# Adaptive max pooling: a nine-row ring, 48 KB load runs issued alternately from SyncE and ScalarE, 9 KB store runs, two early from GpSimd and the rest written last

## Chip, cores, metric

One core of one Trainium2 chip. The metric is the device time in microseconds; lower is better. Ratios are the mean time of one kernel's fast runs over that of the other's of the same rounds, so not quite the ratio of the medians that are quoted beside them. "Span" is the length of the profiled execution; the timed runs are about 2 us longer.

## The reference

```python
x: (32, 256, 4096) float32, output_size = 256
for i in range(256):
    result[:, :, i] = max(x[:, :, 16*i : 16*(i+1)], axis=-1)
```

There are 8192 rows of 16 KB. One "row" below means one row in each of the 128 partitions (2 MB), so the job is 64 such rows, 134.2 MB in and 8.4 MB out. Nothing is reused.

## The kernel before

Each load brings two rows (4 MB, 32 KB per partition) into one of three buffers. VectorE reduces each row in one instruction. The last four rows come in smaller loads with buffers of their own. Of 32 stores (256 KB each, 2 KB runs), 16 are kept back and queued on SyncE behind the body's loads, in three portions.

```python
for n in range(n_body):                              # 30 double rows
    t = in_pool.tile([P, R, O, W], fp32, tag="in")   # 3 buffers
    nc.sync.dma_start(out=t, in_=xt[n])
    o = new_out()
    for r in range(R):
        nc.vector.reduce_max(out=o[:, r*O:(r+1)*O], in_=t[:, r], axis=X)
    out_tiles[n] = o
    if n >= defer_start: deferred.append(n)
    else:                nc.scalar.dma_start(out=ot[n], in_=o)
emit_deferred(6)
# ... two single rows; 5 deferred stores; two rows in quarters; 5 deferred stores; the last store
```

Of the kernel before, what the change touches and what calls it, by code (L numbers as in the profile page):

```python
# [1 line left out]

# [4 lines left out]


@with_exitstack  # L10
def kernel(
    ctx: ExitStack,
    tc: tile.TileContext,
    x: bass.AP,
    output_size: bass.AP,
    out: bass.AP,
):
    nc = tc.nc

    B, C, L = x.shape  # L20
    O = int(output_size)
    assert L % O == 0, (L, O)
    W = L // O

    P = nc.NUM_PARTITIONS

    xf = x.flatten_outer_dims()
    of = out.flatten_outer_dims()
    rows = xf.shape[0]
    assert rows % P == 0  # L30

    fp32 = mybir.dt.float32

    R = 2
    IN_BUFS = 3
    CHUNKS_PER_ROW = 4
    N_CHUNK_ROWS = 2
    N_FULL_ROWS = 2
    DEF_A = 6
    DEF_B = 5  # L40
    DEF_C = 5

    while R > 1 and rows % (P * R) != 0:
        R //= 2
    nprow = rows // P
    nmacro = nprow // R
    n_chunks = CHUNKS_PER_ROW if O % CHUNKS_PER_ROW == 0 else 1
    oc = O // n_chunks

    n_tail_prow = min(N_CHUNK_ROWS + N_FULL_ROWS, nprow)  # L50
    n_chunk_prow = min(N_CHUNK_ROWS, n_tail_prow)
    n_tail_macro = -(-n_tail_prow // R)
    n_body = nmacro - n_tail_macro
    tail_start_prow = n_body * R
    n_defer = min(DEF_A + DEF_B + DEF_C, max(n_body - 1, 0))

    xt = xf.rearrange("(n p r) (o w) -> n p r o w", p=P, r=R, w=W)
    ot = of.rearrange("(n p r) m -> n p (r m)", p=P, r=R)

    in_pool = ctx.enter_context(tc.tile_pool(name="inpool", bufs=IN_BUFS))  # L60
    out_pool = ctx.enter_context(
        tc.tile_pool(name="outpool", bufs=min(nmacro, n_defer + 5))
    )

    out_tiles = {}
    deferred: list[int] = []

    def new_out():
        return out_pool.tile([P, R * O], fp32, tag="out", name="o")

    def emit_deferred(k):
        for _ in range(k):
            if deferred:
                m = deferred.pop(0)
                nc.sync.dma_start(out=ot[m], in_=out_tiles[m])  # L75

    defer_start = n_body - n_defer
    for n in range(n_body):
        t = in_pool.tile([P, R, O, W], fp32, tag="in")
        nc.sync.dma_start(out=t, in_=xt[n])  # L80
        o = new_out()
        for r in range(R):
            nc.vector.reduce_max(  # L83
                out=o[:, r * O : (r + 1) * O],
                in_=t[:, r],
                axis=mybir.AxisListType.X,
            )
        out_tiles[n] = o
        if n >= defer_start:
            deferred.append(n)  # L90
        else:
            nc.scalar.dma_start(out=ot[n], in_=o)

    emit_deferred(DEF_A)

    o = None
    last_n = nmacro - 1
    for q in range(tail_start_prow, nprow):
        n, r = divmod(q, R)
        if r == 0 or o is None:  # L100
            o = new_out()
            out_tiles[n] = o
        if q == nprow - n_chunk_prow:
            emit_deferred(DEF_B)
        if q < nprow - n_chunk_prow:
            tr = in_pool.tile([P, 1, O, W], fp32, tag="inrow", bufs=2)
            nc.sync.dma_start(out=tr, in_=xt[n][:, r : r + 1])
            nc.vector.reduce_max(  # L108
                out=o[:, r * O : (r + 1) * O],
                in_=tr[:, 0],  # L110
                axis=mybir.AxisListType.X,
            )
        else:
            for c in range(n_chunks):
                tl = in_pool.tile(
                    [P, oc, W], fp32, tag="inchunk", bufs=2 * n_chunks
                )
                nc.sync.dma_start(
                    out=tl, in_=xt[n][:, r, c * oc : (c + 1) * oc, :]
                )  # L120
                nc.vector.reduce_max(  # L121
                    out=o[:, r * O + c * oc : r * O + (c + 1) * oc],
                    in_=tl,
                    axis=mybir.AxisListType.X,
                )
        if r == R - 1 and n != last_n:
            nc.scalar.dma_start(out=ot[n], in_=o)

    emit_deferred(len(deferred))

    nc.scalar.dma_start(out=ot[last_n], in_=out_tiles[last_n])


# [1 line left out]
_INS = ['x', 'output_size']  # L135
_OUTS = [((32, 256, 256), 'float32')]
#: Inputs that are plain numbers.
_NUMBERS = {'output_size': 256}


# [26 lines left out]
```

## Time and profile before

| | before |
|---|---|
| time, median of 3 runs | 339.17 us |
| span of the profile | 336.9 us |
| moved | 142.6 MB, mean 423 GB/s |
| VectorE busy | 281.0 us |
| last load landed, by the trace's semaphore events | 332.2 us |

These are lines of the page of the kernel before: VectorE's busy time; its busy tenths, those of the DMA engines and the GB/s in 40 slices of the span; the packet count; and the main group of reductions (line, engine, operation, out<-in, count, busy us, ns of one, waiting before it and for what).

```profile
span 336.9 us, 241 instructions
...
DVE 281.0 (83%) x70; POOL 0.2 (0%) x4
...
DVE  0488988888988889888899888888988888898895
...
DMA  7999999999999999999999999999999999999997
GB/s 311 436 436 441 417 454 406 454 409 454 426 430 430 436 428 434 430 430 435 429 438 432 436 432 436 436 436 428 424 436 428 436 412 436 429 414 427 405 414 275
DMA packets 10370, 142.63 MB, mean 423 GB/s; under 512 B 1152, under 2 KB 1152, under 8 KB 6272
...
L83 DVE TENSOR_REDUCE o<-t 128x256 f32<-128x4096 f32 x60 | 262.4, 4414 | 50.5 <-DMA t<-in_x_dram 50.5
...
```

The DMA line is at 9 from the second slice to the last but one: the transfers bound this kernel. The chain of work that ended last seems to say something else, because it alternates between a load and two reductions. This is a piece of it, in order of time (start, us, what):

```profile
...
186.90 8.76 DVE o L83 x2
195.66 0.02 issue
195.67 20.34 DMA t<-in_x_dram
...
216.03 8.76 DVE o L83 x2
...
```

A load is issued when two reductions have freed its buffer, and it lands 20.3 us later. One load takes only 9.7 us of the engines (128 packets of 32 KB, 1213 ns each by the trace's packet records, over 16 engines); the rest of the 20.3 us is time behind the load in front of it. So the chain shows the return of a buffer, and the engines always have a load queued.

The end, in VectorE's timeline (start, us, engine, line, operation, out<-in, count, waiting before it):

```profile
...
318.22 4.42 DVE L108 TENSOR_REDUCE o<-tr 128x256 f32<-128x4096 f32 x1 [0.86 <-DMA tr<-in_x_dram]
322.79 5.00 DVE L121 TENSOR_REDUCE o<-tl 128x64 f32<-128x1024 f32 x4
328.34 5.06 DVE L121 TENSOR_REDUCE o<-tl 128x64 f32<-128x1024 f32 x4 [0.55 <-DMA tl<-in_x_dram]
```

The last two reductions are of the last quarters to land. VectorE ends at 333.4 us, 1.2 us after the last load. This gap is called the *backlog* below.

### The profile page before, as it was taken

The numbers are of one execution on the slowest core, as the hardware profiler recorded it, in microseconds if no ns is written. First come the engines' busy times: TensorE is split into PE (matmuls) and PEld (weight loads), VectorE is DVE, ScalarE is ACT, GpSimd is POOL, SyncE is SP. The second block draws the span as 40 slices with busy tenths as digits, with TensorE's granted clock in tenths as the row PEclk, the third lists the DMA queues.
The fourth block names the chain that finished last, engine by engine and source line by source line (L and its number), as shares of the span: only waits on it lengthen the run. The fifth ranks groups of instructions, "written<-read, shape, count | busy, mean of one in ns | idle before, by whom it ended". The sixth has DMA issues, their size and how long they took to land.

```text
span 336.9 us, 241 instructions
## 1 busy us (share of the span) xinstructions
DVE 281.0 (83%) x70; POOL 0.2 (0%) x4
## 2 busy tenths in 40 slices
DVE  0488988888988889888899888888988888898895
POOL 0000000000000000000000000000000000000000
DMA  7999999999999999999999999999999999999997
GB/s 311 436 436 441 417 454 406 454 409 454 426 430 430 436 428 434 430 430 435 429 438 432 436 432 436 436 436 428 424 436 428 436 412 436 429 414 427 405 414 275
DMA packets 10370, 142.63 MB, mean 423 GB/s; under 512 B 1152, under 2 KB 1152, under 8 KB 6272
## 3 DMA queue, kind: packets, MB, share of 16 engines
q1 hardware_dynamic: 8064, 138.42, 96.1%
q10 hardware_dynamic: 2304, 4.20, 3.2%
q14 instruction: 2, 0.02, 0.0%
HBM read 134.22 MB, written 8.39 MB: 423 GB/s over the span
## 4 chain that ended last, share of the span: by engine, by line
DMA 74%; DVE 24%; SPq 1%; issue 0%; DVEq 0%
DMA t<-in_x_dram 60%; DVE o L83 23%; DMA out_dram<-o 11%; DMA tl<-in_x_dram 3%; DVE o L121 1%; SPq L75 1%; SPq L80 0%; DVEq L83 0%
## 5 line engine op out<-in xcount | busy, mean ns | idle before, releaser
L83 DVE TENSOR_REDUCE o<-t 128x256 f32<-128x4096 f32 x60 | 262.4, 4414 | 50.5 <-DMA t<-in_x_dram 50.5
L121 DVE TENSOR_REDUCE o<-tl 128x64 f32<-128x1024 f32 x8 | 9.8, 1220 | 1.0 <-DMA tl<-in_x_dram 0.6
L108 DVE TENSOR_REDUCE o<-tr 128x256 f32<-128x4096 f32 x2 | 8.8, 4420 | 1.0 <-DMA tr<-in_x_dram 0.9
L148 POOL MEMSET const-bfloat16-1.0<- 128x1 bf16 x1 | 0.1, 102 | 0.0
L148 POOL MEMSET const-uint8-127<- 128x1 uint8 x1 | 0.1, 101 | 0.0
L148 POOL MEMSET const-float32-0.0<- 128x1 f32 x1 | 0.1, 99 | 0.2 <-issue 0.2
L148 POOL MEMSET const-float32-1.0<- 128x1 f32 x1 | 0.1, 98 | 0.0
## 6 DMA issues: line engine op xcount, KB each, us to landing
t<-in_x_dram SPq DMA_DIRECT2D x30, 4096.0 KB, 21.5
out_dram<-o ACTq DMA_DIRECT2D x16, 256.0 KB, 16.1
out_dram<-o SPq DMA_DIRECT2D x16, 256.0 KB, 14.0
tr<-in_x_dram SPq DMA_DIRECT2D x2, 2048.0 KB, 16.4
tl<-in_x_dram SPq DMA_DIRECT2D x8, 512.0 KB, 9.2
```

The costliest lines, as they stand in the source:

```text
L75: nc.sync.dma_start(out=ot[m], in_=out_tiles[m])
L83: nc.vector.reduce_max(out=o[:, r * O : (r + 1) * O], in_=t[:, r], axis=mybir.AxisListType.X,)
L108: nc.vector.reduce_max(out=o[:, r * O : (r + 1) * O], in_=tr[:, 0], axis=mybir.AxisListType.X,)
L121: nc.vector.reduce_max(out=o[:, r * O + c * oc : r * O + (c + 1) * oc], in_=tl, axis=mybir.AxisListType.X,)
L148: nc = _bacc.Bacc("TRN2", target_bir_lowering=False, num_devices=1)
```

## The change

The intent: longer runs (48 KB in, 9 KB out) for fewer packets; a ring of nine rows; load issues spread over two engines; a few early stores moved to GpSimd; the rest of the stores last. The core of it (set-up and the removed code cut):

```diff
-        nc.sync.dma_start(out=t, in_=xt[n])
+    queues = [nc.sync, nc.scalar]
+    for g in range(N_GROUPS):                      # 7 groups of 9 rows
+        sizes = LATE if g == N_GROUPS - 1 else [LOAD] * (G // LOAD)   # LATE = [3,2,2,1,1], LOAD = 3
+        for n in sizes:
+            queue = queues[n_loads % 2]
+            queue.dma_start(out=ring[:, at : at + n], in_=xg[g][:, r : r + n])
+            n_loads += 1
+            for i in range(n):
+                nc.vector.reduce_max(out=o[...], in_=ring[:, at + i], axis=X)
+        if g < N_GROUPS - 1 - HELD:                # HELD = 4
+            nc.gpsimd.dma_start(out=og[g], in_=o)
+        else:
+            held.append((og[g], o))
+    # ... the 64th row, in four pieces, from SyncE ...
+    for i, (dst, src) in enumerate(held):
+        queues[i % 2].dma_start(out=dst, in_=src)
+    nc.scalar.dma_start(out=ol, in_=last_out)
```

More of the change, by code (lines that the diff above doesn't have):

```diff
@@ L18 @@
     nc = tc.nc
+    P = nc.NUM_PARTITIONS
+    fp32 = mybir.dt.float32
     B, C, L = x.shape
@@ L23 @@
     W = L // O
-    P = nc.NUM_PARTITIONS
     xf = x.flatten_outer_dims()
@@ L29 @@
     rows = xf.shape[0]
-    assert rows % P == 0
-    fp32 = mybir.dt.float32
-    R = 2
-    IN_BUFS = 3
-    CHUNKS_PER_ROW = 4
-    N_CHUNK_ROWS = 2
-    N_FULL_ROWS = 2
-    DEF_A = 6
-    DEF_B = 5
-    DEF_C = 5
-    while R > 1 and rows % (P * R) != 0:
-        R //= 2
-    nprow = rows // P
-    nmacro = nprow // R
-    n_chunks = CHUNKS_PER_ROW if O % CHUNKS_PER_ROW == 0 else 1
-    oc = O // n_chunks
-    n_tail_prow = min(N_CHUNK_ROWS + N_FULL_ROWS, nprow)
-    n_chunk_prow = min(N_CHUNK_ROWS, n_tail_prow)
@@ L52 @@
-    n_tail_macro = -(-n_tail_prow // R)
-    n_body = nmacro - n_tail_macro
-    tail_start_prow = n_body * R
-    n_defer = min(DEF_A + DEF_B + DEF_C, max(n_body - 1, 0))
-    xt = xf.rearrange("(n p r) (o w) -> n p r o w", p=P, r=R, w=W)
-    ot = of.rearrange("(n p r) m -> n p (r m)", p=P, r=R)
-    in_pool = ctx.enter_context(tc.tile_pool(name="inpool", bufs=IN_BUFS))
-    out_pool = ctx.enter_context(
-        tc.tile_pool(name="outpool", bufs=min(nmacro, n_defer + 5))
-    )
-    out_tiles = {}
@@ L66 @@
-    deferred: list[int] = []
-    def new_out():
-        return out_pool.tile([P, R * O], fp32, tag="out", name="o")
-    def emit_deferred(k):
-        for _ in range(k):
-            if deferred:
-                m = deferred.pop(0)
-                nc.sync.dma_start(out=ot[m], in_=out_tiles[m])
-    defer_start = n_body - n_defer
-    for n in range(n_body):
-        t = in_pool.tile([P, R, O, W], fp32, tag="in")
-        nc.sync.dma_start(out=t, in_=xt[n])
-        o = new_out()
-        for r in range(R):
-            nc.vector.reduce_max(
-                out=o[:, r * O : (r + 1) * O],
-                in_=t[:, r],
-                axis=mybir.AxisListType.X,
-            )
-        out_tiles[n] = o
-        if n >= defer_start:
-            deferred.append(n)
-        else:
-            nc.scalar.dma_start(out=ot[n], in_=o)
@@ L94 @@
-    emit_deferred(DEF_A)
-    o = None
-    last_n = nmacro - 1
-    for q in range(tail_start_prow, nprow):
-        n, r = divmod(q, R)
-        if r == 0 or o is None:
-            o = new_out()
-            out_tiles[n] = o
-        if q == nprow - n_chunk_prow:
-            emit_deferred(DEF_B)
-        if q < nprow - n_chunk_prow:
-            tr = in_pool.tile([P, 1, O, W], fp32, tag="inrow", bufs=2)
-            nc.sync.dma_start(out=tr, in_=xt[n][:, r : r + 1])
-            nc.vector.reduce_max(
-                out=o[:, r * O : (r + 1) * O],
-                in_=tr[:, 0],
-                axis=mybir.AxisListType.X,
-            )
-        else:
-            for c in range(n_chunks):
-                tl = in_pool.tile(
-                    [P, oc, W], fp32, tag="inchunk", bufs=2 * n_chunks
-                )
-                nc.sync.dma_start(
-                    out=tl, in_=xt[n][:, r, c * oc : (c + 1) * oc, :]
-                )
+    assert rows == 64 * P
@@ new lines @@
+    RING = 9
+    G = 9
+    N_GROUPS = 7
+    LOAD = 3
+    LATE = [3, 2, 2, 1, 1]
+    HELD = 4
+    PIECES = 4
+    pool = ctx.enter_context(tc.tile_pool(name="pool", bufs=1))
+    ring = pool.tile([P, RING, O, W], fp32, tag="ring", name="ring")
+    outs = [
+        pool.tile([P, G * O], fp32, tag=f"out{i}", name=f"out{i}")
+        for i in range(N_GROUPS - 1)
+    ]
+    last_out = pool.tile([P, O], fp32, tag="lastout", name="lastout")
+    main = N_GROUPS * G * P
+    xg = xf[0:main].rearrange("(g p r) (o w) -> g p r o w", p=P, r=G, w=W)
@@ new lines @@
+    og = of[0:main].rearrange("(g p r) m -> g p (r m)", p=P, r=G)
+    xl = xf[main:rows].rearrange("p (o w) -> p o w", w=W)
+    ol = of[main:rows]
+    queues = [nc.sync, nc.scalar]
+    n_loads = 0
+    n_read = 0
+    held = []
+    for g in range(N_GROUPS):
+        o = outs[g % len(outs)]
+        sizes = LATE if g == N_GROUPS - 1 else [LOAD] * (G // LOAD)
+        r = 0
+        for n in sizes:
+            at = n_read % RING
+            queue = queues[n_loads % 2]
+            queue.dma_start(out=ring[:, at : at + n], in_=xg[g][:, r : r + n])
+            n_loads += 1
+            for i in range(n):
@@ L121 @@
                 nc.vector.reduce_max(
-                    out=o[:, r * O + c * oc : r * O + (c + 1) * oc],
-                    in_=tl,
+                    out=o[:, (r + i) * O : (r + i + 1) * O],
+                    in_=ring[:, at + i],
                     axis=mybir.AxisListType.X,
                 )
-        if r == R - 1 and n != last_n:
-            nc.scalar.dma_start(out=ot[n], in_=o)
-    emit_deferred(len(deferred))
-    nc.scalar.dma_start(out=ot[last_n], in_=out_tiles[last_n])
+            n_read += n
@@ new lines @@
+            r += n
+        if g < N_GROUPS - 1 - HELD:
+            nc.gpsimd.dma_start(out=og[g], in_=o)
+        else:
+            held.append((og[g], o))
+    at = n_read % RING
+    oc = O // PIECES
+    for c in range(PIECES):
+        cut = slice(c * oc, (c + 1) * oc)
+        nc.sync.dma_start(out=ring[:, at, cut], in_=xl[:, cut])
+        nc.vector.reduce_max(
+            out=last_out[:, cut], in_=ring[:, at, cut], axis=mybir.AxisListType.X
+        )
+    for i, (dst, src) in enumerate(held):
+        queues[i % 2].dma_start(out=dst, in_=src)
```

## The prediction, as put on record

> **What bounds the kernel now.** The transfers. The page gives 142.6 MB at a mean of 423 GB/s; its slices show DMA at 9 from the second to the last but one; the stretch view gives 431 GB/s from 20 to 160 us and 430 from 190 to 290. VectorE works 281.0 of 336.9 us; its 50.5 us of waiting are for loads. The chain names a load 22 us, then two reductions 8.76 us, but that is the release of a buffer: 22 us is two loads of 9.7 us and the rest of a third, so a full load is always queued. The Trainium skill ("DMA: Bandwidth & Descriptors", Where 436 GB/s comes from) states a ceiling of 435 GB/s; this trace agrees, at 432. So about 1% is to be had.
>
> **What a packet costs.** Medians in the trace: 32 KB 1213 ns, 16 KB 611, 4 KB 159, 2 KB 84, semaphore 9. They fit 9 ns + bytes / 27.2 GB/s. A 48 KB packet is then an estimated 1815 ns, a 9 KB one 348.
>
> **Sum over 16 engines.** Before: 3840 x 1213 + 256 x 611 + 1024 x 159 + 4096 x 84 + semaphores = 333 us. After: 2304 x 1815 + 128 x (1815 + 2 x 1213 + 2 x 611) + 512 x 159 + 896 x 348 + the last 1 KB runs = 330.4 us. Saved: 2.8 us, all critical, as the engines never idle. But 14 of the 32 stores already alternated on a second queue with load packets, and three loads with their stores took 30.95 us where the sum says 31.2 (without stores 29.1): overlap between queues already hides their 9 ns. That takes 1 us off the saving; two load queues may give as much back.
>
> **What else moves.**
> - Start: loads 0 and 1, on two queues, share the engines packet by packet, so both land at about 32 us, not one at 13. VectorE starts then; its 281 us still end before the loads. Ring slots come free after three reductions (13.2 us), at about 45.5 us; load 2 ends near 46.4, and issue to first packet takes 1.2 us. Gap of 0 to 1.5 us, once. Later VectorE (13.2 per 14.5 us load) gains ground; no further gaps.
> - End: before, the last stores trickle: engines lose 1.4 us in the last 3. After, the stores of groups 4 and 6 (1.18 MB, 2.8 us each) are still queued when the last piece is reduced, so the small last store hides. Gain about 1 us.
> - VectorE's work is unchanged: 64 rows at 4.41 us. The two GpSimd stores are early and hidden.
>
> **Prediction.** 339.2 - 1.8 (packets) + 0.7 (start gap) - 1.0 (end) - 1.0 (two load queues) = 336.0 us (rounded). Range 334.0 to 339.5. Chances: faster by over 2%: 0.02; within 2%: 0.93; slower: 0.05.
>
> **What would show each step.** 48 KB packets near 1815 ns, 9 KB near 348. First reduction near 32 us, not 13.3. One dip in the slices near 45 us. Mid-kernel 432 to 435 GB/s. No slice at the end as low as 275 GB/s. VectorE idle about 50 us still, mostly before its first reduction.
>
> **What would make it wrong.** If dependencies were kept for the whole ring, loads and reductions would take turns: far above 400 us. If the wider stride between partitions (144 KB, not 32) slowed the memory, the middle would fall below 425 GB/s. If VectorE, started 19 us later, never caught up, slots would come late again and again, and dips would repeat. If the held stores ran ahead of the last loads, the tail would be exposed.

## The result

353.30 us (median of 4 runs, 352.35 to 353.35) against 338.95 us before on the same chip: ratio 1.0415, 95% interval 1.0395 to 1.0434. The change is 4% slower; the prediction was 1% faster, and the time lies outside its range.

The page after, the same lines:

```profile
span 351.5 us, 179 instructions
...
DVE 278.0 (79%) x67; POOL 1.4 (0%) x6
...
DVE  0003999999939799498999905999886999299996
...
DMA  8999899999999899999999999999999999999603
GB/s 358 442 436 436 386 386 419 447 459 424 393 464 447 375 463 442 465 391 414 463 424 410 447 447 442 414 442 442 414 397 479 437 411 447 392 437 417 267 0 149
DMA packets 5041, 142.62 MB, mean 406 GB/s; under 512 B 560, under 2 KB 688, under 8 KB 1200
...
L69 DVE TENSOR_REDUCE out<-ring 128x256 f32<-128x4096 f32 x63 | 273.5, 4410 | 70.8 <-DMA ring<-in_x_dram 70.8
...
```

The packets are as meant: half as many, 5041. The digits of DMA are still 8 or 9 up to the 37th slice, but slice 38 has 6 and slice 39 has 0: the engines stand idle for about 12 us near the end, while VectorE's line is at 9. VectorE is busy a little less (278.0 us) and waits 70.8 us instead of about 52. VectorE's timeline after, one line per stretch without a wait, some stretches left out:

```profile
...
32.50 64.99 DVE L69 TENSOR_REDUCE out<-ring 128x256 f32<-128x4096 f32 x15 [32.50 <-DMA ring<-in_x_dram]
103.09 13.07 DVE L69 TENSOR_REDUCE out<-ring 128x256 f32<-128x4096 f32 x3 [5.60 <-DMA ring<-in_x_dram]
...
163.96 39.03 DVE L69 TENSOR_REDUCE out<-ring 128x256 f32<-128x4096 f32 x9 [1.32 <-DMA ring<-in_x_dram]
214.92 39.03 DVE L69 TENSOR_REDUCE out<-ring 128x256 f32<-128x4096 f32 x9 [11.93 <-DMA ring<-in_x_dram]
...
272.14 26.05 DVE L69 TENSOR_REDUCE out<-ring 128x256 f32<-128x4096 f32 x6 [3.27 <-DMA ring<-in_x_dram]
305.28 39.03 DVE L69 TENSOR_REDUCE out<-ring 128x256 f32<-128x4096 f32 x9 [7.09 <-DMA ring<-in_x_dram]
344.23 4.59 DVE L86 TENSOR_REDUCE lastout<-ring 128x64 f32<-128x1024 f32 x4
```

Every bracket is a wait for a load. The first is 32.5 us long; before it was 13.3. Later ones are up to 11.9 us. From 305.28 us on VectorE never waits again, yet it needs 43.5 us more, for the nine rows of the last group and the four pieces, and the last load lands at 333.6 us.

| | before | after | difference |
|---|---|---|---|
| last load landed | 332.2 | 333.6 | +1.4 |
| backlog: from there to VectorE's end | 1.2 | 15.2 | +14.0 |
| from VectorE's end to the end of the span | 3.5 | 2.7 | -0.8 |
| span | 336.9 | 351.5 | +14.6 |

So the transfers did not become slow. The same bytes arrived almost at the same time, but in an order that left VectorE with 15 us of work after the last of them.

A second thing stands out. The source puts the stores of groups 2 to 6 after the last load. These are all the lines of the trace's timeline that issue them (start, us, issuing queue):

```profile
...
162.67 0.35 SPq L91 DMA_DIRECT2D out_dram<-out  x1
...
203.02 0.37 ACTq L91 DMA_DIRECT2D out_dram<-out  x1
...
253.97 0.34 SPq L91 DMA_DIRECT2D out_dram<-out  x1
...
298.23 0.37 ACTq L91 DMA_DIRECT2D out_dram<-out  x1
...
344.34 0.34 SPq L91 DMA_DIRECT2D out_dram<-out  x1
...
```

Four of the five go out as soon as their group is reduced, before the last load. The built program shows why. This is its order on the two issuing engines (12288, 8192, 4096 and 1024 are elements per partition, so 48, 32, 16 and 4 KB; x6 means six in a row; out_61 to out_64 are groups 2 to 5, out_59 is group 6):

```
SyncE:   ring<-x 12288 x6, out_61, ring<-x 12288 x3, out_63, ring<-x 12288, ring<-x 8192, ring<-x 4096, ring<-x 1024 x4, out_59
ScalarE: ring<-x 12288 x7, out_62, ring<-x 12288 x2, ring<-x 8192, ring<-x 4096, out_64, lastout
```

The build has moved three stores, those of groups 2, 3 and 4, ahead of loads that the source has before them. The fourth early one, of group 5, stands where the source has it, behind ScalarE's last load; it is early only because the loads after it are SyncE's. In the kernel before, the built order is that of the source.

### The profile page after: what moved, and what is told of

The parts are those of the page before. It is cut to its first block, busy times and chain, and to the rows that moved or that the text cites. A ratio compares the mean times of both kernels' runs of the same rounds, so it can differ in the third digit from the quotient of the medians.

```text
span 351.5 us, 179 instructions
## 1 busy us (share of the span) xinstructions
DVE 278.0 (79%) x67; POOL 1.4 (0%) x6
## 2 busy tenths in 40 slices
DMA packets 5041, 142.62 MB, mean 406 GB/s; under 512 B 560, under 2 KB 688, under 8 KB 1200
## 3 DMA queue, kind: packets, MB, share of 16 engines
q10 hardware_dynamic: 2016, 65.41, 43.5%
## 4 chain that ended last, share of the span: by engine, by line
DMA 55%; DVE 41%; DVEq 1%; issue 1%
DMA ring<-in_x_dram 55%; DVE out L69 40%; DVE lastout L86 1%; DVEq L123 1%; DVEq L69 0%
## 5 line engine op out<-in xcount | busy, mean ns | idle before, releaser
L69 DVE TENSOR_REDUCE out<-ring 128x256 f32<-128x4096 f32 x63 | 273.5, 4410 | 70.8 <-DMA ring<-in_x_dram 70.8
L86 DVE TENSOR_REDUCE lastout<-ring 128x64 f32<-128x1024 f32 x4 | 4.6, 1208 | 0.0
L77 POOL DMA_DIRECT2D out_dram<-out x2 | 1.2, 599 | 115.4 <-DVE out L69 115.4
## 6 DMA issues: line engine op xcount, KB each, us to landing
ring<-in_x_dram SPq DMA_DIRECT2D x10, 6144.0 KB, 32.8
```

What stands on the lines that cost most here:

```text
L69: nc.vector.reduce_max(out=o[:, (r + i) * O : (r + i + 1) * O], in_=ring[:, at + i], axis=mybir.AxisListType.X,)
L77: nc.gpsimd.dma_start(out=og[g], in_=o)
L86: nc.vector.reduce_max(out=last_out[:, cut], in_=ring[:, at, cut], axis=mybir.AxisListType.X)
```

## The theories

1. **Sharing.** With loads on two queues the engines serve both heads in turn, packet by packet. The load that VectorE needs next gets half the rate, and the one after it gets the other half. Loads land in pairs and late; VectorE waits, and the missing work turns up as a backlog.
2. **Early stores.** The stores that the source holds back go out among the loads. They delay the loads, and nothing is left to fill the DMA engines during the backlog.
3. Rivals: the late start of VectorE alone; the size of the loads (6 MB in three slots); slower memory because of the wider stride between partitions.

The trace alone rules out the slower memory: the median 48 KB packet took 1815 ns, as estimated from 9 ns + bytes / 27.2 GB/s, and between 60 and 300 us both kernels moved 432 GB/s.

It also shows the sharing at the start. These are the DMA queues in the first 34 us (packets, MB, share of 16 engines; q1 is fed by SyncE, q10 by ScalarE):

```profile
...
q1 hardware_dynamic: 176, 7.86, 55.1%
q10 hardware_dynamic: 144, 6.29, 42.7%
...
```

Each 6 MB load is 128 data packets and 16 semaphore writes, so 144. In this stretch q1 finished load 0 and began on load 2, and q10 finished load 1. Loads 0 and 1 landed at 32.48 and 32.65 us, 0.17 us apart. The starts of the packets change between the queues at the pace of one packet per engine: 16 of q1 start between 1.8 and 2.9 us, 16 of q10 between 4.1 and 4.9, 16 of q1 between 5.9 and 6.7, 16 of q10 between 7.7 and 8.6.

The Trainium skill ("DMA: Bandwidth & Descriptors", Queues, rings and completion order) says that each engine "round-robins between the queue rows it has work for, at *packet* granularity", and that it typically drains about 9 to 17 descriptors from one before it switches. The round robin agrees. The grain here is one run of 48 KB: a load has 8 runs and one semaphore write per engine, so with 9 or more at a turn load 0 would have landed some 14 us before load 1 (an estimate: 8 x 1815 ns).

## Experiments

Each edit is shown against the change, unless its heading names another kernel or it repeats the trial above it. Lines that only note the last load or define a name are left out.

### All loads on SyncE, stores as early as in the change (one_early)

```diff
-            queue = queues[n_loads % 2]
+            queue = nc.sync
-        queues[i % 2].dma_start(out=dst, in_=src)
+        (nc.sync if i == HELD else nc.scalar).dma_start(out=dst, in_=src)
```

> Only the loads' queue is undone: all loads on SyncE; the stores of groups 2 to 5 still go out as soon as each group is reduced (all from ScalarE). Theory 1 (two load queues share the engines packet by packet, so the load that is needed next lands late, VectorE starves and carries a backlog past the last load): first reduction near 17.7 us instead of 32.5, VectorE's waiting down from 70.8 to about 58 us, backlog after the last load down from 15 to about 7 us, time 339 to 343 us. Theory 2 (the four stores that the source puts last are placed among the loads by the build, so they take 4 x 2.7 us from the loads and leave nothing to cover the backlog): nothing of that is undone here, time stays near 351 to 353 us.

Measured: 342.52 us, ratio to before 1.0098 (1.0075 to 1.0122). First reduction 18.3 us, waiting 59.1 us, backlog 7.1 us. This is theory 1; theory 2 alone (351 to 353) falls. Its timeline at the end:

```profile
...
294.02 21.73 DVE L69 TENSOR_REDUCE out<-ring 128x256 f32<-128x4096 f32 x5 [1.57 <-DMA ring<-in_x_dram]
...
316.11 17.40 DVE L69 TENSOR_REDUCE out<-ring 128x256 f32<-128x4096 f32 x4 [0.37 <-DMA ring<-in_x_dram]
333.43 4.59 DVE L86 TENSOR_REDUCE lastout<-ring 128x64 f32<-128x1024 f32 x4
...
```

### Two load queues, stores tied behind the last load (two_held)

```diff
-        queues[i % 2].dma_start(out=dst, in_=src)
+        with tc.issue_after(last_on[i % 2].ins):      # last load on that queue
+            queues[i % 2].dma_start(out=dst, in_=src)
```

> Only the order is undone: both load queues stay, but the stores of groups 2 to 6 are tied behind the last load of their queue, as the source has them. Theory 2: the loads end about 10 us sooner (323 us), the stores cover VectorE's backlog, time 336 to 340 us, although the first reduction stays at 32.5 us. Theory 1 alone: time stays above 346 us. If both halves are needed for the loss (they meet in one backlog), this and the run with one queue are each most of the way back.

Measured: 342.13 us, ratio 1.0088 (1.0063 to 1.0113). The last load landed at 327.5 us, backlog 10.0 us; the first reduction was still at 32.8 us. So theory 2 is true as well, and a first reduction at 32 us can be lived with. The time is 2 us above the expected range and the last load 4.5 us later than expected: the stores of groups 3 and 5, tied behind ScalarE's last load alone, landed at 320.2 and 324.2 us, still ahead of SyncE's last pieces. Theory 1 alone (above 346) falls too.

```profile
...
293.96 39.03 DVE L73 TENSOR_REDUCE out<-ring 128x256 f32<-128x4096 f32 x9 [2.18 <-DMA ring<-in_x_dram]
...
332.91 4.59 DVE L90 TENSOR_REDUCE lastout<-ring 128x64 f32<-128x1024 f32 x4
...
```

### Both undone (one_held), and once more with five rounds (one_held_again)

```diff
-            queue = queues[n_loads % 2]
+            queue = nc.sync
-        queues[i % 2].dma_start(out=dst, in_=src)
+        with tc.issue_after(last_on[0].ins):          # the last piece
+            nc.sync.dma_start(out=dst, in_=src)
```

> Both undone: all loads on SyncE, and the stores of groups 2 to 6 behind the last load on SyncE. Both theories: 334.5 to 337.5 us, so about 1% under the kernel before; first reduction 17.7 us, last load landed near 320 us, DMA at 9 to the last but one slice. Near 345 us or above would refute both and leave the 6 MB loads in three slots, or the wider stride, as the cause.

> The version that beat both, once more with five rounds: 336.5 to 337.5 us, 0.5 to 0.8% under the kernel before.

Measured: 337.06 us, ratio 0.9937 (0.9910 to 0.9965); again: 336.94 us, ratio 0.9948 (0.9934 to 0.9962). It beats both kernels; the kernel before by only 0.5 to 0.6%, but both intervals exclude 1. VectorE's end and the page's DMA lines:

```profile
...
285.70 39.03 DVE L70 TENSOR_REDUCE out<-ring 128x256 f32<-128x4096 f32 x9 [1.56 <-DMA ring<-in_x_dram]
...
324.65 4.59 DVE L87 TENSOR_REDUCE lastout<-ring 128x64 f32<-128x1024 f32 x4
...
```

```profile
...
DMA  9999999999998999899998999999989999999997
GB/s 358 393 469 422 422 463 399 462 398 390 469 457 387 428 457 464 387 469 440 405 463 381 469 446 399 463 399 452 457 387 469 434 411 434 434 431 409 401 431 307
...
```

Now the last slice of DMA is the only one below 8: the stores run while VectorE works off its 9 us of backlog. The ring, the 48 KB runs and the stride are the same as in the change, so none of them is the cause.

**What the four together say.** The last group's first load (rows 54 to 56) sets VectorE's end: after it VectorE has 43.5 us of work, with no further wait in three of the runs and one of 0.4 us in the fourth.

| loads | stores of groups 2-5 | VectorE starts row 54 | VectorE ends | span | time |
|---|---|---|---|---|---|
| two queues | early (the change) | 305.28 | 348.8 | 351.5 | 353.30 |
| one queue | early | 294.02 | 338.0 | 340.7 | 342.52 |
| two queues | held | 293.96 | 337.5 | 340.2 | 342.13 |
| one queue | held | 285.70 | 329.2 | 335.2 | 337.06 |

- In the first three, the span ends 2.7 us after VectorE. In the fourth it would be 331.9 us by VectorE, but the held stores land last, at 334.0 us, and the span ends at 335.2: 3.3 us of slack.
- Either part alone makes row 54 start 8.3 us later, and adding the other makes it 11.3 us later again. That sums to 19.6 us; less the slack, 16.3 us, which is the difference of the spans (351.5 - 335.2).
- The 8.3 us of the stores is the time of three of them: 128 packets x 347 ns / 16 engines = 2.8 us each, for groups 2, 3 and 4.
- The 8 to 11 us of the queues are mostly one load that was served too soon. In the change, rows 57 and 58 (9.7 us of the engines) landed only 2.6 us after rows 54 to 56. An estimate: at half rate 1.3 us of it was left, so 8.4 us had been given to it. With two queues and held stores they landed 7.3 us after, so 6.1 us. The remaining 2 or 3 us are not itemised. One more delay can be seen in the trace of the change: the store of group 4 stands just ahead of rows 54 to 56 in SyncE's queue. Its packets run from 269.2 to 281.7 us, 12.5 us for 2.8 us of engine time, because each takes its turn with a 48 KB packet of ScalarE's load. The load of rows 54 to 56 was issued at 268.9 us, and its packets start from 279.2 us on. How much of the 2 or 3 us this makes was not separated.

### One word changed: all loads on SyncE (one_queue)

```diff
-            queue = queues[n_loads % 2]
+            queue = nc.sync
```

> One word of the source changed: every load on SyncE. The built order then has the stores of groups 2 and 4 after the last load on SyncE by itself, those of groups 3 and 5 go early from ScalarE. Theory 1 and 2 together: 335.5 to 339 us, last load near 325 us, backlog 7 us, covered by the two late stores. Theory 2 alone (two of four stores early): about 345 us.

Measured: 337.10 us, ratio 0.9939 (0.9916 to 0.9962). As soon as all loads are on one engine, the build leaves the stores of groups 2 and 4 behind the last load by itself. So this one word undoes the first fault wholly and the second for two of the three stores that had moved, and the time is that of one_held.

### The start in order, the rest alternating (start_in_order, start_pinned)

```diff
-            queue = queues[n_loads % 2]
+            queue = nc.sync if n_loads < 3 else queues[n_loads % 2]
```

> The change as it is, but its first three loads all on SyncE; from the fourth on the loads alternate. If the late start of VectorE (32.5 us instead of 13.3) were the cause: first reduction near 17.7 us and the time about 338 us. Theory 1 (the sharing goes on through the whole run): first reduction near 17.7 us, but VectorE soon waits for a load that shares the engines with the next one; waiting in total still near 70 us, time 350 to 355 us.

Measured: 357.91 us, ratio 1.0563 (1.0545 to 1.0582), above both ranges, with the first reduction at 18.0 us. This run proved less than was meant. In its built program one of VectorE's reductions, of the fourth load, stands ahead of those of the third. So VectorE waited for the fourth load (landed at 63.4 us) while the third (59.8 us) already lay there, a ring slot came free late, and the DMA queues ran empty between 76.1 and 80.8 us. The order of the reductions in all other variants of the change was checked and is that of the source. The trial was repeated with it tied:

```diff
-                nc.vector.reduce_max(...)
+                with tc.issue_after(last_reduce.ins):   # from the second one on
+                    last_reduce = nc.vector.reduce_max(...)
```

> The change, its first three loads all on SyncE, the rest alternating, and VectorE's reductions tied in the order of the source. If the late start were the cause: about 340 us. Theory 1 (sharing goes on to the end): first reduction near 18 us, then waits for loads 2 and 3, row 54 again starting near 305 us, time 350 to 355 us.

Measured: 351.68 us, ratio 1.0382 (1.0365 to 1.0399). The first reduction came at 18.1 us, 14.4 us sooner than in the change, and the time fell by only 1.6 us. The late start is not the cause. VectorE's end:

```profile
...
303.73 39.03 DVE L71 TENSOR_REDUCE out<-ring 128x256 f32<-128x4096 f32 x9 [7.08 <-DMA ring<-in_x_dram]
342.67 4.59 DVE L94 TENSOR_REDUCE lastout<-ring 128x64 f32<-128x1024 f32 x4
```

Row 54 again starts after 303 us, and again 43.5 us follow.

### Loads of one row (fine_loads, fine_to_the_end)

```diff
-    LOAD = 3
+    LOAD = 1
```

> The change as it is, but loads of one row (2 MB, 16 KB runs) instead of three; two queues and the early stores stay. If 6 MB loads in three slots were the cause: 337 to 341 us. Theory 1: the two heads of the queues still share, and the queue that is not needed still takes half; the time stays at 349 to 356 us, although the first reduction comes near 12.5 us.

Measured: 358.78 us, ratio 1.0590 (1.0574 to 1.0606), above the range of theory 1, and far from that of the rival. The first reduction came at 12.9 us. VectorE's timeline near the end:

```profile
...
278.34 8.75 DVE L69 TENSOR_REDUCE out<-ring 128x256 f32<-128x4096 f32 x2 [1.06 <-DMA ring<-in_x_dram]
310.28 39.03 DVE L69 TENSOR_REDUCE out<-ring 128x256 f32<-128x4096 f32 x9 [23.19 <-DMA ring<-in_x_dram]
349.23 4.59 DVE L86 TENSOR_REDUCE lastout<-ring 128x64 f32<-128x1024 f32 x4
```

With small loads most of VectorE's waits after the first were of 1.0 to 1.7 us; two were of 3.1 and 3.4 us, and one of 8.7 us at 202 us, to which the next trial comes back. Then it waited 23.2 us for the last group's first load, which still has three rows. That load, on SyncE, was issued at 257.7 us and landed at 310.2; the load of the *next* two rows, on ScalarE, was issued at 267.5 and landed at 290.9, 19 us sooner. So the landing order was reversed. The load on SyncE also had the store of group 4 (issued at 249.0 us, landed at 290.7) ahead of it. And the last group had kept its sizes 3, 2, 2, 1, 1, so the size of loads was not tested to the end. The second trial does that:

```diff
-    LATE = [3, 2, 2, 1, 1]
+    LATE = [1] * 9
```

> The change with loads of one row throughout, the last group too; two queues and early stores stay. The two heads are then 2 MB each, so the load that is needed can lose at most one row's time (4.9 us) to the other: backlog about 8 us, time 340 to 345 us (16 KB runs cost 2.6 us of it). If sharing harmed whatever the size: 350 us or more, as with fine_loads (358.8).

Measured: 347.16 us, ratio 1.0249 (1.0234 to 1.0265): between the two expectations, 2.2 us above the upper one of theory 1.

```profile
...
296.02 8.75 DVE L69 TENSOR_REDUCE out<-ring 128x256 f32<-128x4096 f32 x2 [8.78 <-DMA ring<-in_x_dram]
305.76 8.74 DVE L69 TENSOR_REDUCE out<-ring 128x256 f32<-128x4096 f32 x2 [1.00 <-DMA ring<-in_x_dram]
316.19 21.73 DVE L69 TENSOR_REDUCE out<-ring 128x256 f32<-128x4096 f32 x5 [1.69 <-DMA ring<-in_x_dram]
337.83 4.59 DVE L86 TENSOR_REDUCE lastout<-ring 128x64 f32<-128x1024 f32 x4
```

Backlog 8.7 us instead of 15.2. So the harm of sharing does grow with the size of the loads that share: 6.1 us of the time come back, although the short runs cost 2.6 us. Sharing and load size are one cause here, not two: with one queue, the large loads do no harm (one_held). One long wait near the end shows, 8.8 us at 296 us. The load it is for was issued on SyncE at 249.6 us, right behind the store of group 4 (249.2), and landed at 295.9; the load of the row after it, on ScalarE, landed at 286.3. The wait of 8.7 us at 202 us, in this run and in fine_loads, is of the same kind: here the load behind the store of group 2 on SyncE landed at 202.3 us, the row after it, on ScalarE, at 192.7. A store in a load queue holds back the loads behind it, while the other queue's loads pass. This one I had not foreseen.

### 16 KB runs instead of 48 KB, all else as in one_held (one_held_16k)

```diff
-    LOAD = 3
+    LOAD = 1
```

> As the run with one load queue and the stores held (337.1 us), but loads of one row: 16 KB runs. It measures what the long runs are worth alone: 3456 more packets... counted as 54 x 128 packets of 16 KB in place of 18 x 128 of 48 KB, that is 4608 packets more at 9 ns over 16 engines = 2.6 us, and 36 more load completions. Expected 339.5 to 340.5 us.

Measured: 339.65 us, ratio 1.0027 (1.0012 to 1.0042), which is 2.6 us over one_held (in another set of rounds; before was 339.17 in the one and 338.71 us in the other, so by the ratios it is 3.0 us). The count in the text that counts is 54 x 128 - 18 x 128 = 4608 packets; the "3456" ahead of it is a slip. The long runs are worth what their packets say.

### Two busy load queues, but both heads of the same load (split_loads)

```diff
-            queue.dma_start(out=ring[:, at : at + n], in_=xg[g][:, r : r + n])
+            for k in range(2):                        # halves of each partition's run
+                cut = slice(k * half, (k + 1) * half)
+                last_on[k] = queues[k].dma_start(out=to[:, cut], in_=of_x[:, cut])
```

The stores are held as in two_held.

> Two load queues that are both busy, but every load is cut in two halves of each partition's run (24 KB each), the first half from SyncE, the second from ScalarE; stores held behind the last loads. Theory 1 says that two queues harm only because the heads are different loads: here both heads are of the same load, so it lands in order; first reduction near 17 us, waiting near 49 us, time 334 to 337.5 us. If two load queues harm by themselves (switching between them, or contention): 340 us or more. If queues that alternate hide the 9 ns of each packet, this is the fastest, near 334.5 us.

Measured: 338.52 us, ratio 0.9992 (0.9976 to 1.0007), outside the range of theory 1 by 1 us and under the rival's 340.

```profile
...
272.06 13.07 DVE L74 TENSOR_REDUCE out<-ring 128x256 f32<-128x4096 f32 x3 [1.54 <-DMA ring<-in_x_dram]
286.77 39.03 DVE L74 TENSOR_REDUCE out<-ring 128x256 f32<-128x4096 f32 x9 [1.64 <-DMA ring<-in_x_dram]
325.72 4.59 DVE L91 TENSOR_REDUCE lastout<-ring 128x64 f32<-128x1024 f32 x4
```

VectorE starts rows 51 and 54 at regular steps of 14.7 us, and row 54 at 286.77, only 1.1 us later than with one queue. The two halves of a load landed 0.2 us apart. So two load queues do no harm by being two; they do harm by having different loads at their heads. The run costs about 1.5 us over one_held (1.9 us by the ratios), and it has 3312 packets more (8353 against 5041): at 9 ns over 16 engines that is 1.9 us. So queues that alternate hide little or nothing of the 9 ns of large packets.

### One queue for the last five loads only (tail_in_order)

```diff
-            queue = queues[n_loads % 2]
+            queue = queues[n_loads % 2] if n_loads < 18 else nc.sync
-        queues[i % 2].dma_start(out=dst, in_=src)
+        (nc.sync if i == HELD else nc.scalar).dma_start(out=dst, in_=src)
```

> The change with its two load queues for the first 18 loads and its four early stores (all from ScalarE), but the five loads of the last group all on SyncE, ahead of the last pieces. If the loss is made by the order in which the last loads land (VectorE's backlog past the last load): backlog 7 to 9 us instead of 15, time 341 to 344 us, the same as with one load queue all along (342.5), although the first reduction stays at 32.5 us. If the waits of VectorE earlier in the run are what costs: 348 us or more.

Measured: 347.18 us (345.88 to 347.76), ratio 1.0243 (1.0221 to 1.0266). It lies between the two expectations: 6.1 us of the 10.8 us that one queue for all loads gains come back.

```profile
...
286.76 52.01 DVE L69 TENSOR_REDUCE out<-ring 128x256 f32<-128x4096 f32 x12 [1.45 <-DMA ring<-in_x_dram]
...
338.69 4.60 DVE L86 TENSOR_REDUCE lastout<-ring 128x64 f32<-128x1024 f32 x4
...
```

Here VectorE's last wait is one load earlier, for rows 51 to 53, which still came from ScalarE: 286.76 + 52.01 + 4.60 = 343.4. With one queue all along that load landed 7 us sooner. So it is not the last five loads alone that decide, but whichever load near the end is late against the work that remains behind it.

### The kernel before with two load queues (before_two_loads), and its control (before_pool_stores)

```diff
-        nc.sync.dma_start(out=t, in_=xt[n])
+        start(n % 2, out=t, in_=xt[n])                # SyncE, ScalarE in turn, source order kept
-            nc.scalar.dma_start(out=ot[n], in_=o)
+            nc.gpsimd.dma_start(out=ot[n], in_=o)     # the control has this edit alone
```

> The other way round: the kernel before, with its 30 double-row loads alternately from SyncE and ScalarE in the source's order, its early stores from GpSimd (so that they don't block ScalarE's queue) and its 16 deferred stores still behind the loads. If two load queues harm any kernel of this kind: 344 us or more. If they harm only where a backlog past the last load results: the last four rows here are on SyncE alone, in small loads with buffers of their own, so the backlog stays at 2 us or so and the time within 1% of before (336 to 342 us), although the first reduction comes near 22 us instead of 13.3.

> Control for the run before this: only the early stores of the kernel before go from GpSimd instead of ScalarE. Expected the same as before within 0.5%: 338 to 341 us.

Measured: 340.43 us, ratio 1.0051 (1.0035 to 1.0066); the control 339.20 us, ratio 1.0018 (1.0001 to 1.0035). The first reduction came at 22.5 us instead of 13.0, but the backlog stayed at 1.2 us. Its last four rows come in small loads on SyncE alone, with buffers of their own, and its 16 stores are still behind the loads; which of these keeps the backlog small was not tested apart. The same two queues that cost 5 to 11 us in the change cost about 1 us here. Early stores from GpSimd cost next to nothing.

## Why the prediction was wrong

- **Right:** transfers bound the kernel before; the 48 KB packet (1815 ns measured and estimated) and the 9 KB packet (347 against 348); the worth of long runs by packet count (one_held_16k); loads 0 and 1 landing together at about 32 us; a small gap near 45 us (0.8 us of engine time lost between 40 and 50 us). VectorE's waiting was foreseen as about 50 us and was 70.8.
- **The step that failed:** "VectorE starts then; its 281 us still end before the loads", with "Later VectorE (13.2 per 14.5 us load) gains ground; no further gaps". The sharing was seen for loads 0 and 1 and then forgotten. It goes on: each load shares the engines with the next. VectorE waited another 38.3 us after its first reduction, and it ended 15.2 us *after* the last load. The comparison of 281 us of work with 330 us of transfers says nothing about the end; what counts there is the landing time of each late load plus the work behind it.
- **A second step that failed:** "After, the stores of groups 4 and 6 (1.18 MB, 2.8 us each) are still queued when the last piece is reduced". I took the order of the source for the order of the program. The build had moved three of the five held stores among the loads, and group 5's went out before SyncE's last loads; group 4's landed at 282.2 us. So nothing covered the backlog, since group 6's store has to wait for VectorE itself (issued at 344.3 us), and the last loads came later (two_held: 6.1 us sooner when held). The prediction had named both dangers under what would make it wrong, that VectorE never catches up and that held stores run ahead of the last loads, but gave neither a place in its sum.
- **A third, small:** "two load queues may give as much back", 1.0 us of the sum. split_loads shows little or nothing of it.
- The rest of the sum was about right as a whole, though its terms were not all measured one by one: with one queue and the stores held the kernel takes 337.06 us, where the sum without the third term, and without the gap at the start that one queue does not have, gives 336.4.

What stays open: why the build orders the stores so when the loads are on two engines and not when they are on one; and 2 to 3 us of the cost of the sharing.

## What to carry to other kernels

Several load queues are not several channels: the engines serve their heads in turn, so a load that is not yet needed takes about half the rate of the one that is, and a store among the loads of one queue lets the other queue's loads pass. Keep loads that are used in order on one queue, or split each load over both. And compare averages only for the middle of a kernel: its end is the largest, over the late loads, of landing time plus work still behind it, and a store held back to cover it must be looked for in the built program or the trace, not in the source.

## What the Trainium skill lacked or had wrong

- "DMA: Bandwidth & Descriptors", Rules for kernel authors, says that spreading DMAs over SP, ACT and GpSimd "Doesn't help — they all run on the same 16 DMA engines and interleave". It does not say that it can harm, by delaying the load that is needed next: 353.30 us with two load queues, 342.52 with one (stores early in both), 342.13 and 337.06 (held).
- The same page, Queues, rings and completion order, gives about 9 to 17 descriptors as typical for a turn of the round robin. With runs of 48 KB a turn was one run: loads of 8 runs per engine on two queues landed 0.17 us apart after 32 us.
- The same page, Why small descriptors are slow, gives a packet overhead of about 3 cycles and works it out for a 256-byte descriptor; it has no time for long ones. Here a packet took bytes / 27.2 GB/s + 9 ns from 2 KB to 48 KB, and 4608 packets more cost 2.6 us in total.
- No page was found that says that the built order of DMA issues can differ from the source's. Here three stores moved, which cost 11.2 us with two load queues (353.30 against 342.13).
